# The causal mask of the diagonal score blocks, moved from TensorE to VectorE in a hybrid SSD and latent-attention kernel

## The chip, the cores and the metric

The kernel runs on one core of one Trainium2 chip. The metric is the device time of one execution in microseconds (us); the number of a kernel is the median of its runs. For the kernel before it is 1918.3 us, the median of three runs of 1915.88 to 1923.65.

## The reference, cut to what matters

The program is one inference step of a two-layer decoder trunk. The first layer is a Mamba-2 (SSD) mixer, the second a multi-head latent attention (MLA) with 16 heads. Both process a prompt of 1024 tokens and a sample group of 8 sequences with 8 new tokens each. The change touches the prompt's attention only, which in the reference is

```python
def latent_partial(q_lat, q_pe, ckv, kpe, mask):
    s = (jnp.einsum('bqhc,bkc->bhqk', q_lat, ckv.astype(F32))
         + jnp.einsum('bqhr,bkr->bhqk', q_pe.astype(F32), kpe.astype(F32))) * MLA_SCALE
    if mask is not None:
        s = jnp.where(mask, s, NEG_INF)
    m = jnp.max(s, axis=-1)
    p = jnp.exp(s - m[..., None])
    return m, jnp.sum(p, axis=-1), jnp.einsum('bhqk,bkc->bhqc', p, ckv.astype(F32))
```

called with the causal mask `q_pos >= k_pos`. A key later than its query must not count.

## The kernel before, in words

All matrix products run in fp32r, a rounded 32-bit type. To keep fp32 accuracy each operand is split into a rounded high part and a low remainder, and a product is made of three: high by high, high by low and low by high.

The program has these stages: the SSD layer, the projections of the MLA layer (`mla_in`, `mla_q`), the attention of the prompt head by head (`mla_heads`), and the sample group with the output projection (`mla_sample`). The change lies in the third.

`mla_heads` (L1492) loops over the 16 heads. A head has two query halves (`qc`, 512 queries each) and per half its key blocks of 128 (`jb`): 4 blocks for the first half, 8 for the second, 12 steps in all, `t` = 0 to 11. In each step it calls

- `qk` (L1424) for block `t`: three products into one of two PSUM buffers "st" (`HB[0]` is 2), scores with keys on the partitions and queries along the free axis. The query operand carries two more rows, minus the row maximum, so that the scores come out already shifted. Then two exponentials on ScalarE read that buffer: `th` (L1445), rounded to fp32r, and `P` (L1446), in fp32. Then `tl = P - th` (L1448) is the remainder of the probabilities. It is computed on GpSimd for odd `jb` and on VectorE for even `jb`.
- some units of other work: the row maxima of the next head (`maxpass`, L1390: one product "sc" and one masked maximum on VectorE, L1405 or L1407), and the preparation of the head after that (`prep`: transposes and splits of queries; for even heads keys too, and for every fourth head the values of four heads). These share four PSUM buffers "sc".
- `pv` (L1451) for the block two steps earlier (`LEAD` is 2): three products L1465, L1466, L1467 with the values, of which the third needs `tl`. After the last block of a half, ScalarE makes the reciprocal of the row sums as an exponential of a logarithm (`rl`, L1475 and L1477), VectorE multiplies by the gate (`og`, L1476), and GpSimd multiplies both (`og`, L1478). Because of the lead, the second half of a head ends in step `t` = 1 of the next head.

Where `jb >= 4 * qc` the key block meets the diagonal. Only the queries from its first key on are computed, so the four diagonal blocks of a half have 512, 384, 256 and 128 columns, and the first 128 columns need the causal mask. A head has 8 diagonal blocks. The mask, 0 or -1e30, is added by a fourth product (L1441), the identity times the mask, accumulated into the same buffer. Its two operands `mr` are rounded copies, made once in `Heads.start` (L1206, L1207).

The order of TensorE and GpSimd in this stage is that of the program text (`manual_schedule` in `layer_mla`). VectorE, ScalarE and the DMA queues get their order from the framework's scheduler when the program is built; each engine then runs its queue in that order.

Of the kernel before, what the change touches and what calls it, by code (L numbers as in the profile page):

```python
# [9 lines left out]
F32R = mybir.dt.float32r  # L10
AF = mybir.ActivationFunctionType
ALU = mybir.AluOpType
# [30 lines left out]
LEAD = 2  # L43
PF = 4
HB = (2, 4, 1, 2)
MDVE = False
SB = {"tr": 4, "sc4": 2, "on": 1, "pj": 1}
QG = 2
PRE = 4
# [66 lines left out]
def open_pool(tc, name, bufs=1, space=None, **kw):  # L116
    if space is None:
        return tc.tile_pool(name=name, bufs=bufs, reuse_waits="tile", **kw)
    if space == PS:
        return tc.tile_pool(name=name, bufs=bufs, space=space, reuse_waits="tile", **kw)  # L120
    return tc.tile_pool(name=name, bufs=bufs, space=space, **kw)
# [456 lines left out]
def bass_window(acc, start, stride, n):  # L578
    a = acc[:, :, start : start + (NB - 1) * stride + n]
    return bass.AP(a.tensor, a.offset, [list(a.ap[0]), list(a.ap[1]), [stride, NB], [1, n]])  # L580
# [572 lines left out]
def mla_q(k, st):  # L1153
    tc, nc, I = k.tc, k.nc, k.I
    wuq = I["mla_w_uq"][0].rearrange("q h e -> q (h e)")
    wp = st.enter_context(open_pool(tc, name="wpq", bufs=1, side="right"))
    sp = st.enter_context(open_pool(tc, name="spq", bufs=1, side="right"))
    ct, sn = k.rope
    for c in range(4):
        cs = slice(384 * c, 384 * c + 384)  # L1160
        wh, wl = load_w(k, wp if c % 2 else k.wu, wuq[:, cs], 4, 384, "wq", 1, k.wu, 1) if c else k.wu0
        for i, (t0, m) in enumerate(TILES):
            qt = sp.tile([128, 4, 96], F32, tag="qt", name=f"qt{c}{i}", bufs=2)
            qf = qt.rearrange("p h e -> p (h e)")
            p = k.psum.tile([128, 512], F32, tag="pj", name=f"pq{c}{i}", bufs=PB["pj"])
            drain(mm_tok(nc, p, m, 384, [(*both(k.cqh, k.cql, i, kk), wh[:, kk], wl[:, kk]) for kk in range(4)]))
            if m == 64:
                fold(nc, qf, p, 384)
            else:
                nc.scalar.copy(qf[:m], p[:m, :384])  # L1170
            u = sp.tile([128, 4, 2, 16], F32, tag="u3", name=f"u3{c}{i}", bufs=2)
            w = sp.tile([128, 4, 2, 16], F32, tag="w3", name=f"w3{c}{i}", bufs=2)
            cb = bass_bcast2(ct[:m, i], 4, 2)
            sb = bass_bcast2(sn[:m, i], 4, 2)
            pe = qt[:m, :, 64:96].rearrange("p h (a e) -> p h a e", a=2)
            nc.vector.tensor_tensor(u[:m], pe, cb, op=ALU.mult)
            nc.vector.tensor_tensor(w[:m], pe, sb, op=ALU.mult)
            nc.vector.tensor_tensor(pe[:, :, 0], u[:m, :, 0], w[:m, :, 1], op=ALU.subtract)
            nc.vector.tensor_tensor(pe[:, :, 1], u[:m, :, 1], w[:m, :, 0], op=ALU.add)
            nc.sync.dma_start(k.q_d[t0 : t0 + m, cs], qf[:m])  # L1180
            yield


class Heads:
# [16 lines left out]
        self.add_q(vp, 1)  # L1201

    def start(self, st):
        k, nc = self.k, self.k.nc
        self.sp = st.enter_context(open_pool(k.tc, name="q0", bufs=1))
        nc.vector.tensor_copy(k.mr[:, 0:128], k.ident)  # L1206
        nc.vector.tensor_copy(k.mr[:, 128:], self.maskt)  # L1207
        self.identr, self.masktr = k.mr[:, 0:128], k.mr[:, 128:]

    def load_mask(self):  # L1210
        nc = self.k.nc
# [212 lines left out]
    def qk(self, h, qc, jb):  # L1424
        k, nc, sp = self.k, self.k.nc, self.sp
        qh, ql = self.q_of(h)
        kh, kl = self.kT[h % NKT]
        o = max(0, jb - 4 * qc) * 128
        n = 512 - o
        ks = slice(128 * jb, 128 * jb + 128)  # L1430
        qs = slice(512 * qc + o, 512 * qc + 512)
        ps = self.psum.tile([128, 512], F32, tag="st", name=f"st{h}_{qc}_{jb}", bufs=HB[0])
        diag = jb >= 4 * qc
        nc.tensor.matmul(ps[:, :n], kh[:, ks], qh[:, qs], start=True, stop=False)  # L1434
        nc.tensor.matmul(ps[:, :n], kh[:, ks], ql[:, qs], start=False, stop=False)  # L1435
        nc.tensor.matmul(ps[:, :n], kl[:, ks], qh[:, qs], start=False, stop=MDVE or not diag)  # L1436
        if diag:
            if MDVE:
                nc.vector.tensor_tensor(ps[:, :128], ps[:, :128], self.maskt, op=ALU.add)
            else:  # L1440
                nc.tensor.matmul(ps[:, :128], self.identr, self.masktr, start=False, stop=True)  # L1441
        th = sp.tile([128, 512], F32R, tag="th", name="th", bufs=4)
        tl = sp.tile([128, 512], F32R, tag="tl", name="tl", bufs=3)
        P = sp.tile([128, 512], F32, tag="P", name="P", bufs=3)
        nc.scalar.activation(th[:, :n], ps[:, :n], AF.Exp, scale=SCALE)  # L1445
        nc.scalar.activation(P[:, :n], ps[:, :n], AF.Exp, scale=SCALE)  # L1446
        eng = nc.gpsimd if jb % 2 else nc.vector
        eng.tensor_tensor(tl[:, :n], P[:, :n], th[:, :n].bitcast(F32), op=ALU.subtract)  # L1448
        return th, tl

# [414 lines left out]
def mla_sample(k, sm, flow):  # L1865
    with ExitStack() as st:
        psum = st.enter_context(open_pool(k.tc, name="ps4", bufs=1, space=PS))
        out = MlaOut(k, st, psum, sm)
        sm.open(st, psum, out)
        sm.late_open(st)  # L1870
        k.sm = sm
        out.fill = fill = out.pieces(range(8))
        next(fill)
        drain(flow)
        last = None
        for x in TAIL:
            if x == "a":
                sm.turn_acc(NB - 1)
            elif x == "f":
                last = out.pieces((8,), sm.finish())  # L1880
            else:
                next(last if x == "s" else fill, None)
        drain(fill)
        drain(last)
# [138 lines left out]
def layer_mla(k):  # L2023
    tc, nc = k.tc, k.nc
    k.og_d = k.dram.tile([8, 128, SEQ], F32, name="og_d")
    k.npool = k.I["cache_ckv"].shape[1]
    with ExitStack() as st:
        k.q_d = k.dram.tile([T, MH * 96], F32, name="q_d")
        PB.update(PB2)
        k.cm = st.enter_context(open_pool(tc, name="cm", bufs=1))  # L2030
        right, mid, heads, k.mps = ExitStack(), ExitStack(), ExitStack(), ExitStack()
        p2 = ExitStack()
        k.psum = p2.enter_context(open_pool(tc, name="ps2", bufs=1, space=PS))
        k.psum.tile([128, 512], F32, tag="y", name="y2", bufs=PB["y"])
        mla_in(k, right, mid)
        k.qp = qp = st.enter_context(open_pool(tc, name="qp", bufs=1))
        k.qlh = qp.tile([128, 2, NB, 128], F32R, name="qlh")
        k.qll = qp.tile([128, 2, NB, 128], F32R, name="qll")
        k.qpr = qp.tile([96, NB, 128], F32R, name="qpr")
        k.mr = qp.tile([128, 256], F32R, name="mr")  # L2040
        early = ExitStack()
        hd = Heads(k, early)
        q0 = ExitStack()
        hd.start(q0)
        early_units = [hd.prep_kv(0)] * 13 + [hd.prep_q(0)] * 5 + [hd.maxpass(0, 0)] * 6
        early_units += [hd.prep_q(1)] * 5 + [hd.maxpass(0, 1)] * 10
        done = 0
        for n, _ in enumerate(mla_q(k, mid)):
            if n == 32:
                tc.keep_in_program_order(nc.scalar.preload_act_table_set("natural_log_exp_and_others"))  # L2050
            while done < min((n - Q0 + 1) * len(early_units) // (33 - Q0), len(early_units)):
                next(early_units[done], None)
                done += 1
        q0.close()
        mid.close()
        p2.close()
        psum = heads.enter_context(open_pool(tc, name="ps3", bufs=1, space=PS))
        hd.open(heads, psum)
        sm = Sample(k)
        with tc.manual_schedule(engines={nc.tensor.engine, nc.gpsimd.engine}):  # L2060
            flow = mla_heads(k, hd, sm, early, st)
        heads.close()
        right.close()
        with tc.manual_schedule(engines={nc.tensor.engine, nc.gpsimd.engine}):
            mla_sample(k, sm, flow)
        k.mps.close()
# [33 lines left out]
def hybrid_kernel(tc, ins, outs):  # L2100
    k = Ctx()
    k.tc, k.nc, k.I, k.O, k.ng = tc, tc.nc, ins, outs, G
    with ExitStack() as st:
        setup(k, st)
        layer_ssd(k)
        layer_mla(k)
# [19 lines left out]
```

## Time and profile before

| | |
|---|---|
| median of 3 runs | 1918.3 us |
| profiled execution, span | 1915.0 us |
| TensorE (PE) busy | 1887.4 us |
| VectorE (DVE) busy | 1208.5 us |
| ScalarE (ACT) busy | 1101.1 us |
| GpSimd (POOL) busy | 823.3 us |
| fourth product L1441 | 128 times, from 1309.6 to 1651.5 us |

The profile is of one execution. Its span runs from the first to the last instruction of the program; the time of a run also has what lies around it. A row of the lines view has the line, the engine, the operation, the tiles written and read, the shapes and the count, then the busy time, the mean of one in ns, and the idle time of the engine just before it with what ended that idle time. A row of the timeline has the start, the duration, the engine, the line and the tiles. PE is the matrix products and PEld the loads of their stationary operand. Products are pipelined, so that the duration of one is longer than the time until the next can start.

### The profile page before, as it was taken

To read this page: it belongs to the slowest core of one execution; us is meant where nothing else is said; L and a number is where in the kernel's file an instruction comes from. 1 tells how busy PE (TensorE), PEld (TensorE's weight loads), DVE (VectorE), ACT (ScalarE), POOL (GpSimd) and SP (SyncE) were. 2 spreads that over 40 slices of the span, in tenths; PEclk is the share of its full clock that TensorE was granted. 3 is DMA by queue.
4 is the path that set the end of the run, shared out by engine and by line. 5 is a ranking of instruction groups with operands and counts; after the bars stand their busy time and mean duration, and the time that the engine had idled before them with its cause. 6 is when DMAs were issued, how large, how long until landed. Compare 5 with 4: busy or idle time off the path is not lost.

```text
span 1915.0 us, 33672 instructions
## 1 busy us (share of the span) xinstructions
PE 1887.4 (99%) x12023; PEld 1728.1 (90%) x12023; DVE 1208.5 (63%) x2500; ACT 1101.1 (57%) x2528; POOL 823.3 (43%) x1116
## 2 busy tenths in 40 slices
PE   8999999999999999999999999999999999999998
PEld 7999999999999999888788998898888887888887
DVE  5557676757676767765534214566887878666665
ACT  6467666767666666732214323436777777755552
POOL 2447555555655555453004322103443434764551
PEclk9999999999999999999999999999999999999999
DMA  5223323332323232644424662233111112664451
GB/s 165 54 79 91 94 83 94 88 106 83 101 84 99 85 99 78 212 158 175 166 110 133 209 226 75 69 110 95 47 52 41 53 41 58 228 204 142 146 170 37
DMA packets 183967, 212.51 MB, mean 111 GB/s; under 512 B 19148, under 2 KB 147928, under 8 KB 182776
## 3 DMA queue, kind: packets, MB, share of 16 engines
q1 hardware_dynamic: 177304, 185.32, 31.1%
q0 software_dynamic: 6416, 24.91, 3.8%
q8 instruction: 95, 1.56, 0.3%
q14 instruction: 72, 0.59, 0.1%
q10 hardware_dynamic: 80, 0.13, 0.0%
HBM read 151.76 MB, written 58.52 MB: 110 GB/s over the span
## 4 chain that ended last, share of the span: by engine, by line
PE 90%; DMA 3%; DVE 3%; ACT 3%; issue 1%; POOL 0%; SPq 0%; POOLq 0%; DVEq 0%; ACTq 0%
PE pj L89 24%; PE pz L101 8%; PE pq L101 6%; PE pob L101 5%; PE p L101 5%; PE poa L101 4%; PE py L640 3%; PE sc L89 3%; PE o L89 2%; PE sc L1402 2%; PE o L1465 2%; PE o L1467 2%; PE st L1434 2%; PE st L1435 2%; PE st L1436 2%; PE o L1466 2%
## 5 line engine op out<-in xcount | busy, mean ns | idle before, releaser
L89 PE MATMUL pj<-xl,wih 128*128 128x384 f32 (+1 forms) x768 | 255.4, 333 | 0.0
L89 PE MATMUL pj<-xh,wih 128*128 128x384 f32 (+1 forms) x768 | 252.9, 333 | 1.2 <-ACT xh L276 0.8
L89 PE MATMUL pj<-xh,wil 128*128 128x384 f32 (+1 forms) x768 | 252.9, 329 | 0.0
L1448 POOL TENSOR_TENSOR tl<-P,th 128x384 fp32r<-128x384 f32 (+1 forms) x96 | 90.6, 944 | 232.3 <-ACT P L1446 186.6
L528 DVE SCALAR_TENSOR_TENSOR acc<-raw,vec,acc 128x1112 f32<-128x1112 f32 x96 | 141.6, 1476 | 15.3 <-ACT acc L524 14.4
L89 PEld LDWEIGHTS pj<-xh,wih 128*128 128x128 f32 x768 | 143.8, 188 | 2.6 <-ACT xh L276 1.4
L89 PEld LDWEIGHTS pj<-xl,wih 128*128 128x128 f32 x768 | 144.5, 188 | 1.0
L89 PEld LDWEIGHTS pj<-xh,wil 128*128 128x128 f32 x768 | 144.5, 188 | 0.5
L101 PE MATMUL pz<-wih,xh 128*128 128x256 f32 x504 | 143.3, 288 | 1.4 <-ACT z L569 1.4
L101 PE MATMUL pz<-wil,xh 128*128 128x256 f32 (+1 forms) x504 | 139.8, 283 | 0.0
L1445 ACT ACTIVATE th<-st 128x512 fp32r<-128x512 f32 x192 | 94.6, 493 | 66.6 <-PE st L1441 50.9
L101 PE MATMUL pz<-wih,xl 128*128 128x256 f32 x448 | 128.5, 287 | 0.0
L1733 POOL TENSOR_TENSOR kvl<-pgr,kvh 128x256 fp32r<-128x256 f32 x128 | 97.8, 791 | 70.6 <-ACT kvh L1731 70.3
L635 ACT ACTIVATE M<-M,tok 128x128 f32<-128x128 f32 (+1 forms) x288 | 90.4, 386 | 51.4 <-DVE M L631 51.2
L136 DVE TENSOR_TENSOR wil<-wraw,wih 128x512 fp32r<-128x512 f32 x88 | 74.4, 851 | 38.2 <-ACT wih L130 31.7
L101 PEld LDWEIGHTS pz<-wih,xh 128*128 128x128 f32 x504 | 95.9, 190 | 2.3 <-ACT z L569 1.8
L1446 ACT ACTIVATE P<-st 128x512 f32<-128x512 f32 x192 | 93.5, 487 | 0.0
L101 PEld LDWEIGHTS pz<-wil,xh 128*128 128x128 f32 (+1 forms) x504 | 92.8, 184 | 0.1
L101 PE MATMUL p<-w,oh 128*128 128x512 f32 (+3 forms) x304 | 88.8, 386 | 0.6 <-DVE h L1983 0.6
L616 POOL TENSOR_TENSOR xdd<-xsT,tok 128x256 f32<-128x256 f32 x64 | 50.0, 781 | 86.4 <-ACT xsT L602 83.3
L101 PEld LDWEIGHTS pz<-wih,xl 128*128 128x128 f32 x448 | 85.4, 191 | 0.7
L1448 DVE TENSOR_TENSOR tl<-P,th 128x512 fp32r<-128x512 f32 x96 | 72.1, 752 | 18.9 <-ACT P L1446 18.7
(830 smaller groups left out, 6212.5 us busy)
## 6 DMA issues: line engine op xcount, KB each, us to landing
wraw<-in_ssd_w_in SPq DMA_DIRECT2D x92, 256.0 KB
M<-acs_d SPq DMA_DIRECT2D x64, 256.0 KB
s<-in_state_ssm SPq DMA_DIRECT2D x32, 256.0 KB
y_d<-y SPq DMA_DIRECT2D x64, 128.0 KB
out_s_ssm<-s SPq DMA_DIRECT2D x32, 256.0 KB
q_d<-qt SPq DMA_DIRECT2D x32, 192.0 KB
qp<-q_d SPq DMA_DIRECT2D x8, 768.0 KB
wraw<-in_ssd_w_out SPq DMA_DIRECT2D x10, 512.0 KB
```

The source lines that it names most:

```text
L89: nc.tensor.matmul(out, a, b, start=(i == 0), stop=(i == n - 1))
L101: nc.tensor.matmul(o, a, b, start=(j == 0), stop=(j == len(ops) - 1))
L136: return (eng or nc.vector).tensor_tensor(lo, src, hi.bitcast(F32), op=ALU.subtract)
L528: last = nc.vector.scalar_tensor_tensor(acc, raw[:, j : j + n], k.convw[j][:, blk : blk + 1], acc, op0=ALU.mult, op1=ALU.add)
L616: nc.gpsimd.tensor_tensor(v3(xdd), v3(xsT), hb(2), op=ALU.mult)
L635: nc.scalar.activation(M[:m, h, :m], M[:m, h, :m], AF.Exp, bias=tk[:, 0, 4 * g + h : 4 * g + h + 1])
L640: nc.tensor.matmul(py[:m, h * 64 : h * 64 + 64], M[:m, h, :m], xsT[:m, h * 64 : h * 64 + 64], start=True, stop=True)
L1402: nc.tensor.matmul(ps[:, :n], qh[:96, 128 * i : 128 * i + 128], kh[:96, 512 * c : 512 * c + n], start=True, stop=True)
L1445: nc.scalar.activation(th[:, :n], ps[:, :n], AF.Exp, scale=SCALE)
L1446: nc.scalar.activation(P[:, :n], ps[:, :n], AF.Exp, scale=SCALE)
L1448: eng.tensor_tensor(tl[:, :n], P[:, :n], th[:, :n].bitcast(F32), op=ALU.subtract)
L1733: nc.gpsimd.tensor_tensor(rl[:, j], raw[:, j], rh[:, j].bitcast(F32), op=ALU.subtract)
```

## The change

The fourth product is gone. The third product ends the group, and VectorE then adds the fp32 mask `maskt`, which was in SBUF already, to the first 128 columns of the scores in PSUM, in place; the exponentials wait for that addition. The rounded copies of identity and mask are no longer made and their tile `mr` (1 KB per partition) is dropped, with the flag that chose between the two ways. The remainders `tl` of all diagonal blocks are computed on GpSimd, those with even `jb` too, which were on VectorE; the other blocks stay as they were.

```diff
@@ class Heads, start
-        k, nc = self.k, self.k.nc
+        k = self.k
         self.sp = st.enter_context(open_pool(k.tc, name="q0", bufs=1))
-        nc.vector.tensor_copy(k.mr[:, 0:128], k.ident)
-        nc.vector.tensor_copy(k.mr[:, 128:], self.maskt)
-        self.identr, self.masktr = k.mr[:, 0:128], k.mr[:, 128:]
@@ class Heads, qk
-        nc.tensor.matmul(ps[:, :n], kl[:, ks], qh[:, qs], start=False, stop=MDVE or not diag)
+        nc.tensor.matmul(ps[:, :n], kl[:, ks], qh[:, qs], start=False, stop=True)
         if diag:
-            if MDVE:
-                nc.vector.tensor_tensor(ps[:, :128], ps[:, :128], self.maskt, op=ALU.add)
-            else:
-                nc.tensor.matmul(ps[:, :128], self.identr, self.masktr, start=False, stop=True)
+            nc.vector.tensor_tensor(ps[:, :128], ps[:, :128], self.maskt, op=ALU.add)
...
-        eng = nc.gpsimd if jb % 2 else nc.vector
+        eng = nc.gpsimd if diag or jb % 2 else nc.vector
         eng.tensor_tensor(tl[:, :n], P[:, :n], th[:, :n].bitcast(F32), op=ALU.subtract)
@@ layer_mla
-        k.mr = qp.tile([128, 256], F32R, name="mr")
```

More of the change, by code (lines that the diff above doesn't have):

```diff
@@ L45 @@
 HB = (2, 4, 1, 2)
-MDVE = False
 SB = {"tr": 4, "sc4": 2, "on": 1, "pj": 1}
```

## The prediction

> **What bounds the kernel now.** I read the page first: the shares of the engines and the chain of work that ended last.
>
> ```profile
> span 1915.0 us, 33672 instructions
> PE 1887.4 (99%) x12023; PEld 1728.1 (90%) x12023; DVE 1208.5 (63%) x2500; ACT 1101.1 (57%) x2528; POOL 823.3 (43%) x1116
> ...
> PE 90%; DMA 3%; DVE 3%; ACT 3%; issue 1%; POOL 0%; SPq 0%; POOLq 0%; DVEq 0%; ACTq 0%
> ```
>
> TensorE is busy for 99% of the span and is 90% of the chain. The change lies in the stage of the attention heads, so I read that stage next: the windows view of the whole stage and of 50 us in its middle (columns: window, length, then busy time and instructions of PE, PEld, DVE, ACT, POOL, then clock and DMA), and the waits of PE in the stage.
>
> ```profile
> 1305.00:1655.00 350.00, 346.90 (x2023) 298.82 (x2023) 276.11 (x679) 264.65 (x599) 156.44 (x153) 1.00 0.22 64
> 1400.00:1450.00 50.00, 49.97 (x302) 43.65 (x301) 41.13 (x103) 39.14 (x89) 20.24 (x20) 1.00 0.18 50
> ```
>
> ```profile
> PE o L1467 <- POOL tl L1448: 1.3, 1, 1.3
> PE o L1467 <- DVE tl L1448: 0.9, 1, 0.9
> ```
>
> PE idles 0.03 us of 50 in mid-stage, at a granted clock of 1.00. Its few waits, 2.2 us in all, are for `tl`, the remainders that the change moves. VectorE is 82% busy (41.13 of 50), ScalarE 78%, GpSimd 40%. So each TensorE product removed shortens the time, and anything that makes `th`, `tl` or a score buffer late by more than its slack lengthens it.
>
> **What the change removes on TensorE.** The mask product runs 128 times (16 heads, 8 diagonal blocks each). What one costs can't be read from its busy time of 0.225 us, since products are pipelined; it is read from the starts. Its row in the tile view of the scores (least, median and largest ns), then the timeline of PE (start, duration): two 512-wide products, a block with the mask, a 128-wide block:
>
> ```profile
> L1441 PE MATMUL st<-mr x128: 221/225/278, 1309.6 to 1651.5; 128*128 128x128 f32 x128
> ```
>
> ```profile
> 1450.20 0.39 PE L1467 MATMUL o<-tl,Vh 128*128 128x512 f32 x1
> 1450.43 0.40 PE L1434 MATMUL st<-qTh,kTh 98*128 98x512 f32 x1
> ...
> 1453.10 0.39 PE L1436 MATMUL st<-qTh,kTl 98*128 98x512 f32 x1
> 1453.33 0.23 PE L1441 MATMUL st<-mr 128*128 128x128 f32 x1
> 1453.40 0.44 PE L89 MATMUL kp<-kvh,w 128*128 128x512 f32 x1
> 1453.68 0.40 PE L89 MATMUL kp<-kvl,w 128*128 128x512 f32 x1
> ...
> 1461.53 0.28 PE L1436 MATMUL st<-qTh,kTl 98*128 98x128 f32 x1
> 1461.64 0.28 PE L1441 MATMUL st<-mr 128*128 128x128 f32 x1
> ```
>
> A 512-wide product takes a slot of 0.23 us (1450.20 to 1450.43). With a mask product behind it, two 512-wide ones that should take 0.46 take 1453.10 to 1453.68, 0.58: the mask costs 0.12, of which 0.07 stands between its own start and the next, and 0.05 in the product after it, which starts late in effect. Among 128-wide products the slot is 0.11. I take 0.11: 128 x 0.11 = 14.1 us. Bounds: 0.07 gives 9.0, 0.12 gives 15.4. The lower one is what the chain counts, from start to start; I don't take it, because the 0.28 slot of the next product shows the rest.
>
> [...]
>
> The two casts that made the constant operands go as well:
>
> ```profile
> L1206 DVE CAST mr<-ident x1: 951/951/951, 1219.2 to 1219.2; 128x128 fp32r<-128x128 f32 x1
> L1207 DVE CAST mr<-mk x1: 1080/1080/1080, 1220.0 to 1220.0; 128x128 fp32r<-128x128 f32 x1
> ```
>
> They took 2.03 us of VectorE in the projections of the queries, and nothing waited for them (the views of these lines name no one). I cost them at nothing: PE was multiplying all through. If that cover were gone they would be worth 2 us, a gain.
>
> **What it adds and moves.** The remainders in the stage, shapes apart (busy time, mean ns), and the masked maxima by their line (least, median and largest ns):
>
> ```profile
> L1448 DVE TENSOR_TENSOR tl<-P,th 128x512 fp32r<-128x512 f32 x64 | 56.3, 880 | 18.8 <-ACT P L1446 18.7
> L1448 POOL TENSOR_TENSOR tl<-P,th 128x512 fp32r<-128x512 f32 x32 | 43.3, 1354 | 44.4 <-ACT P L1446 23.2 <-PE sc L1402 11.0 <-DVE nr L1419 4.5
> ...
> L1448 POOL TENSOR_TENSOR tl<-P,th 128x384 fp32r<-128x384 f32 x32 | 32.3, 1010 | 156.2 <-ACT P L1446 132.3 <-PE o L1467 23.7
> ...
> L1448 DVE TENSOR_TENSOR tl<-P,th 128x256 fp32r<-128x256 f32 x32 | 15.8, 494 | 0.1
> ...
> L1448 POOL TENSOR_TENSOR tl<-P,th 128x128 fp32r<-128x128 f32 x32 | 15.0, 468 | 31.7 <-ACT P L1446 31.1
> ```
>
> ```profile
> L1407 DVE CUSTOM_DVE_ANT_0 sc<-sc,mk x64: 276/490/733, 1259.2 to 1614.4; 128x128 f32<-128x128 f32 x16, 128x256 f32<-128x256 f32 x16, 128x384 f32<-128x384 f32 x16, 128x512 f32<-128x512 f32 x16
> ```
>
> The add of a 128x128 mask in PSUM has no row. The nearest is the narrowest form of L1407, 128x128: PSUM and the SBUF mask in, PSUM out, 0.276 us. I take 0.28. It can't be below nothing, as it is a new instruction; above, the subtraction of twice its width, 0.494. So 128 x 0.28 = 36 us (up to 63) are added to VectorE. Moved from it to GpSimd are the even diagonal blocks, 32 of 512 and 32 of 256: 32 x 0.88 + 32 x 0.494 = 44 us go from VectorE. On GpSimd they cost 32 x 1.354 + 32 x 0.74 = 67 us (0.74 is half way between its 468 at 128 and 1010 at 384). VectorE so loses 8 us (at worst gains 19), GpSimd goes from 156 to 223 of 350: no engine but PE becomes full on average. What counts is the delay in single chains.
>
> Such a chain was: last product, `th`, `P`, `tl`, then the third value product (L1467). Now the add stands before `th`, and `tl` of an even block takes longer. The add waits in VectorE's queue with the splits and maxima that free the four "sc" buffers behind it; `th` waits for it in ScalarE's queue, with the casts and the `rl` exponentials behind; PE waits for these in the end. In program order GpSimd does `tl` of blocks 0 and 1, `og` of the head before (L1478, 1.3 us), then blocks 2 and 3. Head 7, one of those with little preparation, in time order (start, duration):
>
> ```profile
> 1465.59 0.69 DVE L1448 TENSOR_TENSOR tl<-P,th 128x512 fp32r<-128x512 f32 x1 [0.47 <-ACT P L1446]
> ...
> 1466.42 0.34 PE L1434 MATMUL st<-qTh,kTh 98*128 98x256 f32 x1
> ...
> 1467.59 0.40 PE L1467 MATMUL o<-tl,Vh 128*128 128x512 f32 x1
> ...
> 1468.03 0.63 ACT L1477 ACTIVATE rl<-rl 64x512 f32<-64x512 f32 x1
> ...
> 1468.74 1.29 POOL L1478 TENSOR_TENSOR og<-og,rl 64x512 f32<-64x512 f32 x1 [1.14 <-PE sc L1402]
> ...
> 1470.20 0.28 PE L1467 MATMUL o<-tl,Vh 128*128 128x256 f32 x1
> ...
> 1475.28 1.28 POOL L1478 TENSOR_TENSOR og<-og,rl 64x512 f32<-64x512 f32 x1 [1.61 <-ACT rl L1477]
> ...
> 1475.36 1.75 DVE L1448 TENSOR_TENSOR tl<-P,th 128x512 fp32r<-128x512 f32 x1
> ```
>
> Block 0: `tl` ended at 1466.28 and was used at 1467.59, a slack of 1.31. The add (0.28) and GpSimd's 1.29 to 1.35 in place of 0.69 use 0.94; PE comes 0.22 earlier by two mask products gone. Slack left 0.15; I put 0.1 us of stall on each such head for a busy VectorE.
>
> Block 2: its `tl`, an even one, ran on VectorE, free of `og`. On GpSimd it follows `og`, which ends at 1470.03; 0.74 later is 1470.77, and PE wants it at 1470.20, 0.22 earlier by the products gone. That is a stall of 0.6 to 0.8; up to 1.1 if the add also pushes `P` and so the exponential behind it; only about 0.1 if ScalarE's planned order puts that exponential ahead of `th`, which would free `og` some 0.6 us sooner. I take 0.7. In an even head the same pair stands wide apart (head 6, columns as above):
>
> ```profile
> 1441.78 1.43 POOL L1478 TENSOR_TENSOR og<-og,rl 64x512 f32<-64x512 f32 x1 [1.41 <-PE o L1467]
> ...
> 1445.27 0.28 PE L1467 MATMUL o<-tl,Vh 128*128 128x256 f32 x1
> ```
>
> Here 1443.21 + 0.74 leaves over 1 us. So the stall falls on the seven odd heads 1 to 13, 7 x (0.7 + 0.1) = 5.6, and I put the same 0.7 on the two last, which have little to do between blocks: 1.4 (bounds 0, and twice 1.1 and some more for block 0, 3).
>
> The last two rows of head 7 show a VectorE subtraction held by GpSimd: `tl` took 1.75 instead of 0.69 while `og` ran. The add is not priced so: of the 64 masked maxima, with one operand in PSUM, the longest, at four times the width, took 0.733. [...] If the add were held as `tl` was, each would take 1.06 us more; the rows of the maxima speak against it.
>
> **The sum.** -14.1 + 5.6 + 1.4 = -7.1 us: the span goes from 1915.0 to 1907.9. The median of the runs is 1918.3, 3.3 above the profiled span, so 1911.2. A measurement of this kernel can tell about 0.5%, 9.6 us, from no change.
>
> **Rivals.** *The stalls don't come.* The exponential moves ahead, stalls sum to 2 us, and the gain is 12 to 13: 1906. For it: ScalarE has 22% free, and VectorE and ScalarE are planned anew; against: `og` alone takes 1.3 us of GpSimd just there.
>
> *The product was nearly free.* If it costs its 0.07 only, the gain is 9.0 less 7.0, 2 us: 1916. Against it is the 0.28 slot above. [...]
>
> *Slower: the add holds the score buffers.* There are two ("st"); `P` frees one. In head 7 `P` of block 0 ends as its `tl` starts, 1465.59, and block 2 takes the buffer at 1466.42, a slack of 0.83. An add that waits for one running VectorE instruction (0.69) and takes 0.28 is 0.97 late. If PE lost 0.2 us in each of the 128 blocks: 25.6 - 14.1 = +11.5, so 1930. It breaks even at 0.11 a block and is slower by 0.5% from 0.19. For it: VectorE at 82%. Against: in head 7 VectorE stood idle for 0.47 right there.
>
> **How the numbers follow.** Forecast 0.44 (own range 1908.7 to 1914); no stalls 0.35; nearly free 0.09; slower 0.12. So faster by over 0.5% 0.35; within 0.5% 0.53; slower 0.12. The lower end, 1902, is 1918.3 less 15.4 with no stall at all, rounded; the upper, 1925, reaches from the forecast over the nearly free product and half way into the slower rival.
>
> **What would show it.** No L1441 row; 128 VectorE adds of about 0.28 us; the slot after a block's third product 0.23 at once. Right: in odd heads PE waits at L1467 for a GpSimd `tl` behind `og`, 5 to 8 us in all, nearly none elsewhere. Wrong: PE waits at the first score product for `P` (buffers held), PE waits on "sc" buffers, or no waits at L1467.

## The result and the profile after

The changed kernel takes 1925.76 us (median of 5 runs, 1921.4 to 1927.35), the kernel before 1915.88 us in the same comparison (5 runs, 1914.28 to 1923.65). The ratio is 1.0041, with a 95% interval of 1.0025 to 1.0056: slower, though by less than the 0.5% that the prediction named as the limit of what can be told; a gain was forecast. Measured once more against 29 runs of the kernel before, the same program gave 1924.17 us, a ratio of 1.0036 (1.0023 to 1.0048). So about 7 us were lost where 7 were to be gained. One run of an experiment below, of the kernel before with a longer lead, took 3057.74 us at a granted clock of 0.56 and is left out of its median and ratio.

The page of the profile after: span, busy time, and the shares of the chain that ended last.

```profile
span 1925.6 us, 33687 instructions
PE 1884.9 (98%) x11895; PEld 1713.5 (89%) x11895; DVE 1204.7 (63%) x2562; ACT 1095.7 (57%) x2528; POOL 882.2 (46%) x1180
PE 84%; DMA 5%; DVE 4%; ACT 4%; POOL 2%; issue 1%; SPq 0%; POOLq 0%; DVEq 0%; ACTq 0%
```

TensorE is busy for 2.5 us less than before and the span is 10.6 us longer: TensorE waits. Its share of the chain fell from 90% to 84%, and GpSimd, at 0% before, has 2%.

The span needs care. Ahead of the heads both programs are the same but for two casts, yet the first score product of head 0 comes 6.0 us later than in the profile before. In the profiles of the twelve further runs it came 0.8 to 5.0 us later; four of those programs change nothing ahead of the heads, and they come 0.8 to 4.1 us later. So the profile before happens to be an execution that lost little up to there, and most of these 6 us are not the change's. From here on I match the products of both traces in order, from start to start, inside the heads only: by the first score product of the last head, the changed kernel has lost another 6.1 us, and by the last value product of the stage 7.4.

Windows over the stage of the heads and over 50 us of its middle (busy times of PE, PEld, DVE, ACT and POOL, then clock and DMA):

```profile
1315.00:1668.00 353.00, 338.53 (x1870) 280.16 (x1869) 276.27 (x736) 259.18 (x596) 217.52 (x217) 0.99 0.22 62
1412.00:1462.00 50.00, 49.16 (x286) 41.78 (x285) 41.82 (x115) 39.03 (x91) 29.30 (x30) 1.00 0.18 50
```

No engine but PE is full: VectorE 276 of 353 us, GpSimd 218. Yet PE, which idled 0.03 us of 50 in mid-stage before, now idles 0.84. The waits of PE in the stage, and then its products that waited longest, in order of time (in brackets the idle time before the product and who ended it):

```profile
PE o L1460 <- POOL tl L1441: 9.1, 10, 2.8
PE o L1460 <- DVE og L1469: 1.0, 1, 1.0
PE o L1460 <- DVE tl L1441: 1.0, 1, 1.0
PE nkp L1594 <- DVE nk L1591: 0.8, 1, 0.8
PE st L1430 <- ACT P L1439: 0.8, 2, 0.6
```

```profile
1346.56 0.39 PE L1460 MATMUL o<-tl,Vh 128*128 128x256 f32 x1 [2.77 <-POOL tl L1441]
1395.82 0.39 PE L1460 MATMUL o<-tl,Vh 128*128 128x256 f32 x1 [0.77 <-POOL tl L1441]
1436.04 0.39 PE L1460 MATMUL o<-tl,Vh 128*128 128x256 f32 x1 [0.71 <-POOL tl L1441]
...
1609.27 0.39 PE L1460 MATMUL o<-tl,Vh 128*128 128x256 f32 x1 [0.79 <-POOL tl L1441]
1630.03 0.39 PE L1460 MATMUL o<-tl,Vh 128*128 128x256 f32 x1 [1.19 <-POOL tl L1441]
```

These are the third value products of a block of 256 columns, block 2 of the first half: L1460 is the old L1467, `tl` is now L1441. One stands in each odd head, 0.68 to 0.79 us in heads 3 to 13, but 2.77 in head 1. The view of waits understates them. It counts idle time from the modelled end of the product before, 0.39 us after its start, while the next could have started after 0.23; and a wait below that difference of 0.16 isn't listed. From start to start over the whole stage, and without the half clock shown below, the third value products lose 11.8 us against before and the first score products 2.7.

Head 7, in time order, shows the ordinary case (the row ending in "x2" holds the `tl` of blocks 2 and 3):

```profile
1478.52 0.30 DVE L1434 TENSOR_TENSOR st<-st,mk 128x128 f32<-128x128 f32 x1 [0.53 <-PE st L1432]
...
1479.41 0.38 ACT L1439 ACTIVATE P<-st 128x256 f32<-128x256 f32 x1
1479.68 0.62 ACT L1470 ACTIVATE rl<-rl 64x512 f32<-64x512 f32 x1
...
1480.38 1.29 POOL L1471 TENSOR_TENSOR og<-og,rl 64x512 f32<-64x512 f32 x1 [0.60 <-ACT rl L1470]
1481.63 1.13 POOL L1441 TENSOR_TENSOR tl<-P,th 128x256 fp32r<-128x256 f32 x2
1482.40 0.38 PE L1460 MATMUL o<-tl,Vh 128*128 128x256 f32 x1 [0.78 <-POOL tl L1441]
```

`P` of block 2 is ready at 1479.79. GpSimd is idle then, but next in its queue stands `og`, which waits 0.60 us for the exponential `rl` that ScalarE does behind `P`. So `tl` of block 2 starts 1.84 us after its input was there. Head 1 has one thing more:

```profile
1342.01 1.03 POOL L1243 CAST kTh<-kTh 32x1024 fp32r<-32x1024 f32 x1
1342.99 1.03 POOL L1243 CAST kTl<-kTl 32x1024 fp32r<-32x1024 f32 x1
1344.11 1.27 POOL L1471 TENSOR_TENSOR og<-og,rl 64x512 f32<-64x512 f32 x1
1345.35 1.57 POOL L1441 TENSOR_TENSOR tl<-P,th 128x256 fp32r<-128x256 f32 x2
```

Two casts of rope keys (L1243, L1247 in the kernel before), 1.03 us each, stand ahead of `og`. Right behind that wait the granted clock is down, as the window of the next 10 us shows:

```profile
1350.00:1360.00 10.00, 10.00 (x41) 8.03 (x41) 6.07 (x14) 5.91 (x13) 7.06 (x8) 0.77 0.11 28
```

From 1347.8 on the clock is at half (0.50 in the window from 1350 to 1353) for 6.8 us, 4.6 of them in this window. That costs about half of its length, 3.4 us (an estimate). Not all of it is a loss against the kernel before, whose profile has 6.8 us of half clock as well, just behind the heads from 1673.2 on, where the profile after has none. The mean granted clock is 0.9974 over the 11 runs of the changed kernel and 0.9983 over 76 runs of the one before; on 1920 us the difference comes to 1.7 us, again an estimate.

### The profile page after: what moved, and what is told of

Its sections match the earlier page's. It is cut to its first block, busy times and chain, and to the rows that moved or that the text cites. A ratio compares the mean times of both kernels' runs of the same rounds, so it can differ in the third digit from the quotient of the medians.

```text
span 1925.6 us, 33687 instructions
## 1 busy us (share of the span) xinstructions
PE 1884.9 (98%) x11895; PEld 1713.5 (89%) x11895; DVE 1204.7 (63%) x2562; ACT 1095.7 (57%) x2528; POOL 882.2 (46%) x1180
## 4 chain that ended last, share of the span: by engine, by line
PE 84%; DMA 5%; DVE 4%; ACT 4%; POOL 2%; issue 1%; SPq 0%; POOLq 0%; DVEq 0%; ACTq 0%
PE pj L88 24%; PE pz L100 8%; PE pq L100 6%; PE pob L100 5%; PE p L100 5%; PE poa L100 3%; PE py L639 3%; PE sc L88 2%; PE o L88 2%; PE o L1460 2%; PE st L1430 1%; PE o L1458 1%; PE pk L100 1%; PE st L1432 1%; PE st L1431 1%
## 5 line engine op out<-in xcount | busy, mean ns | idle before, releaser
L1441 POOL TENSOR_TENSOR tl<-P,th 128x512 fp32r<-128x512 f32 (+3 forms) x160 | 154.1, 975 | 185.2 <-DVE mx L1403 84.9
L129 ACT CAST wih<-wraw 128x512 fp32r<-128x512 f32 x92 | 55.9, 616 | 45.2 <-PE pj L88 29.5
```

The source lines that it names most:

```text
L129: k.cast = nc.scalar.copy(hi, src)
```

## The experiments

Two theories. A: the loss is `tl` of the diagonal's even blocks, which in GpSimd's fixed order queues behind `og`, and in head 1 behind the key casts. B: the loss is the add. It stands between the scores and both exponentials and takes VectorE's room, so that `P` and VectorE's own results come late. A third question is what the product itself was worth. Ratios are against the kernel before on the same chip.

**The add alone, remainders where they were** (the changed kernel, with):

```diff
-        eng = nc.gpsimd if diag or jb % 2 else nc.vector
+        eng = nc.gpsimd if jb % 2 else nc.vector
```

> Mask added by VectorE, remainders divided as before (odd on GpSimd, even on VectorE). Theory A (the loss comes from even diagonal remainders queued on GpSimd behind og and, in head 1, behind the key casts): 10 to 14 us faster than before, near 1904; PE waits at the third value product fall from 11 us to 2 or 3. Theory B (the loss comes from the add standing before the exponentials): about as slow as the changed kernel, 5 to 10 us slower than before, and PE waits for P at the first score product.

1928.55 us, 1.0061 (1.0048 to 1.0074). A's forecast failed, and B's sign held: the add in place of the product loses without any move to GpSimd. The window of the stage, and the waits:

```profile
1312.00:1668.00 356.00, 338.98 (x1868) 277.39 (x1867) 305.20 (x800) 258.82 (x595) 155.36 (x152) 1.00 0.22 62
```

```profile
PE o L1467 <- DVE tl L1448: 5.6, 10, 0.8
PE nmp L1417 <- DVE nm L1414: 5.3, 13, 0.5
PE st L1434 <- ACT P L1446: 2.8, 7, 0.8
```

VectorE is at 305 of 356 us, 86%, and PE waits for what it makes: its `tl`, the maxima `nm`, and, through the exponentials, `P`.

But this run doesn't price the add, because more than the edit differs. VectorE's order is planned anew for each program. I compared the orders in the stage by the names of the instructions, adds and remainders left out: against the kernel before, 180 of 573 stand in another place here, most of them steps of the row maxima, and 28 in the changed kernel. The waits for `nm` may come from that plan.

**The remainders alone, product kept** (the kernel before, with the opposite edit):

```diff
-        eng = nc.gpsimd if jb % 2 else nc.vector
+        eng = nc.gpsimd if diag or jb % 2 else nc.vector
```

> The fourth product stays, only the even diagonal remainders go to GpSimd. Theory A: 8 to 14 us slower than before (0.6 us in each odd head, 2.5 us in head 1, a clock step of 3 us after it, 2 us in the last heads). Theory B: the same as before within 2 us.

1923.95 us, 1.0037 (1.0022 to 1.0051). PE's waits:

```profile
PE o L1467 <- POOL tl L1448: 5.9, 11, 1.7
```

So the move by itself costs some 7 us, too, and VectorE's order is nearly that of before (8 of 573 elsewhere). A is right about the move. What the add costs, the runs with zeros below tell. The two don't simply add up: the changed kernel has both and lost less than the run with the add alone.

**The mask product twice** (the kernel before; two equal products accumulated, so the mask is added twice):

```diff
-                nc.tensor.matmul(ps[:, :128], self.identr, self.masktr, start=False, stop=True)
+                for z in (False, True): nc.tensor.matmul(ps[:, :128], self.identr, self.masktr, start=False, stop=z)
```

> The mask product is issued twice, 128 products more, nothing else. If one costs 0.11 us of PE: 14 us slower, 12 to 16. If it costs only the 0.07 between the starts: 9 us or less. Either theory of the loss says the same.

1927.12 us, 1.0053 (1.0039 to 1.0067). The timeline of PE at a block with two 512-wide key products behind it:

```profile
1458.82 0.39 PE L1436 MATMUL st<-qTh,kTl 98*128 98x512 f32 x1
1459.06 0.34 PE L1441 MATMUL st<-mr 128*128 128x128 f32 x2
1459.23 0.45 PE L89 MATMUL kp<-kvh,w 128*128 128x512 f32 x1
1459.52 0.40 PE L89 MATMUL kp<-kvl,w 128*128 128x512 f32 x1
```

From 1458.82 to 1459.52 are 0.70 us; with one mask product the same stretch took 0.58, and in the changed kernel, with none, 0.46. So the slot is 0.12 here; in the median over the blocks it is 0.11, as was taken. In time, though, the second product costs 10.2 us (7.5 to 12.8), less than 128 x 0.11: a later PE finds fewer results late, and its third value products lose 3.2 us less by their starts.

**Block 2 back to VectorE** (the changed kernel):

```diff
-        eng = nc.gpsimd if diag or jb % 2 else nc.vector
+        eng = nc.gpsimd if (diag and jb % 4 == 0) or jb % 2 else nc.vector
```

> The changed kernel with the 256-wide diagonal remainders back on VectorE; the 512-wide diagonal ones stay on GpSimd. Theory A: the waits behind og go, 8 to 12 us faster than the changed kernel, 1906 to 1912 where before is 1916; head 1 shows no wait of 2.8 us and no half clock. Theory B: within 2 us of the changed kernel.

1925.41 us, 1.0038 (1.0025 to 1.0051): no better than the changed kernel, so A's forecast failed again. PE's waits:

```profile
PE o L1467 <- POOL tl L1448: 3.6, 4, 1.4
PE o L1467 <- DVE tl L1448: 3.3, 7, 1.0
PE nmp L1417 <- DVE nm L1414: 2.6, 7, 0.5
PE st L1434 <- ACT P L1446: 2.1, 3, 0.9
```

GpSimd's waits fell from 9.1 to 3.6, and VectorE's `tl` and `nm` came in their place. In head 1 A's forecast held: no third value product waits there, and no half clock follows. The queue behind `og` is real, but the work taken back by VectorE makes other results of that engine late.

**`og` later, remainders on GpSimd** (the changed kernel; GpSimd's product and its store are put off to steps 3 and 6):

```diff
-        nc.gpsimd.tensor_tensor(og[pj], og[pj], rl[pj], op=ALU.mult)
-        nc.sync.dma_start(k.og_d[pr, pj, cs], og[pj])
+
+        def late():
+            nc.gpsimd.tensor_tensor(og[pj], og[pj], rl[pj], op=ALU.mult)
+            nc.sync.dma_start(k.og_d[pr, pj, cs], og[pj])
+
+        self.late = late
...
+            if t in (3, 6) and getattr(hd, "late", None):
+                hd.late()
+                hd.late = None
...
+    hd.late()
```

> The changed kernel with og on GpSimd put behind the remainder of block 3 (or of block 6 of the second half) instead of before that of block 2; nothing added or removed. If block 2 was late because of og: the 0.85 us in each odd head go and the wait in head 1 shrinks, 6 to 9 us faster than the changed kernel, 1916 to 1920. If the add or VectorE makes it late: within 2 us of the changed kernel.

1916.3 us, 0.9986 (0.9977 to 0.9995). The same instructions in another order are 8 us quicker by the medians than the changed kernel, 10 by the ratios. Head 7, where the row with "x3" holds three `tl` back to back:

```profile
1467.20 3.09 POOL L1448 TENSOR_TENSOR tl<-P,th 128x512 fp32r<-128x512 f32 x3 [1.76 <-ACT P L1446]
...
1471.13 1.29 POOL L1480 TENSOR_TENSOR og<-og,rl 64x512 f32<-64x512 f32 x1
1471.15 0.28 PE L1467 MATMUL o<-tl,Vh 128*128 128x256 f32 x1
```

Block 2's `tl` is done before `og`, and its product has no wait. VectorE and ScalarE run in the changed kernel's order but for a handful of places, so the gain is that of GpSimd's queue. This shows A for the changed kernel.

**A zero add on top of the kernel before**, of 128 and of 8 columns (product and remainders as before; what is added are zeros):

```diff
                 nc.tensor.matmul(ps[:, :128], self.identr, self.masktr, start=False, stop=True)
+            nc.vector.tensor_tensor(ps[:, :128], ps[:, :128], self.maskr[:, 0:128], op=ALU.add)
```

The narrow one has, in place of the added line:

```diff
+            nc.vector.tensor_tensor(ps[:, :8], ps[:, :8], self.maskr[:, 0:8], op=ALU.add)
```

> The kernel before, fourth product and division of the remainders kept, and VectorE adds zeros to the same 128x128 scores in addition: the price of the add alone. By the prediction's sum it would cost 1 to 3 us (covered). By the run with the mask on VectorE alone, where 24 us were lost against 14 gained, it costs 10 to 18 us: 1927 to 1935.

> As the run that adds zeros to 128 columns, but to 8 columns: the same wait between score and exponential, a third or less of VectorE's time. If the wait in the chain costs: within 3 us of the 128-column run. If VectorE's room costs: at most a third of its loss, 1918 to 1923.

1924.07 us, 1.0028 (1.0019 to 1.0038) with 128 columns, and 1920.62 us, 1.0008 (0.9998 to 1.0018) with 8. The adds in the tile view (least, median, largest ns):

```profile
L1442 DVE TENSOR_TENSOR st<-st,mk x128: 277/299/331, 1313.0 to 1660.7; 128x128 f32<-128x128 f32 x128
```

```profile
L1442 DVE TENSOR_TENSOR st<-st,mk x128: 154/174/213, 1315.1 to 1660.5; 128x8 f32<-128x8 f32 x128
```

The wide add costs 5.4 us (3.6 to 7.3). The narrow one stands in the same place with the same waits, takes 58% of the time, and costs 1.5 (-0.4 to 3.5), which can't be told from nothing. So the price isn't only that of one more step and one more wait between scores and exponentials, which the narrow one has too. A price in proportion to the time of the adds would be 3.1 us for the narrow one, and these runs don't exclude it.

The traces tell more, with one profile of each. From start to start up to the last head, against the kernel before, the first score products, which wait for the exponentials, lose 2.0 us with the wide add and 2.2 with the narrow one. The products that wait for VectorE's maxima and keys ("nmp", "sc", "nkp") lose 3.2 and 0.5, the third value products lose 0.1 and gain 1.6. So what the wide add costs beyond the narrow one is VectorE's results coming late, in other words room on VectorE, of which the wide one takes 37 us and the narrow one 22.

**A longer lead, on the changed kernel and on the one before** (value products come three steps later instead of two; `qsn`, `wt` and `nr` give up their second buffer for the room; in the kernel before, the gate's tile `gt` does so too):

```diff
-LEAD = 2
+LEAD = 3
...
-        th = sp.tile([128, 512], F32R, tag="th", name="th", bufs=4)
-        tl = sp.tile([128, 512], F32R, tag="tl", name="tl", bufs=3)
+        th = sp.tile([128, 512], F32R, tag="th", name="th", bufs=5)
+        tl = sp.tile([128, 512], F32R, tag="tl", name="tl", bufs=4)
```

> The changed kernel with the value products three blocks behind the scores instead of two (one th and one tl buffer more, three small buffers single to make room). It gives tl a step of about 1.8 us more, but leaves the two score buffers as they are. If the loss is tl late at the third value product: those waits of PE (11 us) fall to 1 or 2 and it is 8 to 13 us faster than the changed kernel, 1912 to 1918 beside a before of 1917. If it is the score buffers or VectorE's room: within 3 us of the changed kernel.

> The kernel before with the longer lead alone (three blocks; the small buffers and the gate's single to make room). Its waits at the third value product were 2.2 us, so at most that is to be had: 0 to 3 us faster. If the lead were worth 4 us by itself, the gain of the changed kernel with the longer lead would not be the mask's.

The changed kernel with it: 1913.74 us, 0.9976 (0.9966 to 0.9985), 10 to 12 us below its runs without. The kernel before with it: 1914.88 us, 0.9984 (0.9975 to 0.9993). The waits of PE for GpSimd's `tl`, in the changed kernel and in the one before, both with the longer lead:

```profile
PE o L1467 <- POOL tl L1448: 1.4, 2, 0.8
```

```profile
PE o L1467 <- POOL tl L1448: 2.1, 2, 1.6
```

With one step more of slack these waits of the changed kernel fall from 9.1 us to 1.4, and its median is the lowest of all. But the lead helps the kernel before as well, and the two intervals overlap: that the mask on VectorE gains anything with the longer lead isn't shown.

**Both cures together** (the changed kernel with the longer lead and its buffers, and `og` put off as above, to later steps):

```diff
+            if t in (4, 7) and getattr(hd, "late", None):
+                hd.late()
+                hd.late = None
```

> The changed kernel with both the longer lead and og behind the remainders of the diagonal. With the lead alone 5.7 us were gained in the heads, with og late alone 3.6, of the 14 that the products cost; waits for P at the score buffers (2 to 3 us) stay. If the two cover the same waits: as the longer lead alone, 1913; if they add: 1908 to 1911.

1916.31 us, 0.9991 (0.998 to 1.0001). They don't add up. One wait in head 14 accounts for most of it in the profiled execution, with the half clock that comes with it:

```profile
PE o L1467 <- POOL tl L1448: 4.1, 2, 3.9
```

```profile
1622.16 1.25 POOL L1480 TENSOR_TENSOR og<-og,rl 64x512 f32<-64x512 f32 x1 [4.30 <-DMA pgr<-in_cache_ckv,ptidx]
1623.49 2.49 POOL L1448 TENSOR_TENSOR tl<-P,th 128x512 fp32r<-128x512 f32 x2
...
1624.81 0.79 PE L1467 MATMUL o<-tl,Vh 128*128 128x512 f32 x1 [3.85 <-POOL tl L1448]
```

Here GpSimd issues two gathers of cache pages for the sample group (`pgr`), and the `og` behind them then waits 4.30 us, by the profile until a gather has landed. The remainders stand behind that `og`: again a one-off in GpSimd's queue. The clock goes to half during the wait, at 1623.5, for 6.8 us.

**The changed kernel again, and with head 1's key casts on VectorE:**

```diff
-            (nc.vector if j == 1 else nc.gpsimd).tensor_copy(a[64:96], b[64:96].bitcast(F32))
+            (nc.vector if j in (1, 3) else nc.gpsimd).tensor_copy(a[64:96], b[64:96].bitcast(F32))
```

> The changed kernel once more (same program, lines kept in place). By its first runs 5 to 11 us slower than before; its own profile shows which part of the 6 us lost ahead of the heads, where both programs are the same, is chance.

> The changed kernel with the two casts of rope keys in head 1 (L1247, h = 3) on VectorE instead of GpSimd. If the 2.8 us wait of head 1 came from block 2's remainder queued behind these casts and og: the wait falls to about 0.8 and the half clock of 6.8 us after it goes, 3 to 6 us faster than the changed kernel. If not: within 1 us.

1924.17 us, 1.0036 (1.0023 to 1.0048), and 1921.09 us, 1.0012 (1.0003 to 1.0021). Two casts moved away are worth 3.1 us on the same chip: the wait in head 1 is 0.62 in place of 2.67, and the half clock behind it is gone. The orders of VectorE and ScalarE are otherwise the changed kernel's but for a handful of places. Head 1 with the casts on VectorE:

```profile
1339.79 1.29 POOL L1478 TENSOR_TENSOR og<-og,rl 64x512 f32<-64x512 f32 x1 [0.56 <-ACT rl L1477]
1341.04 1.13 POOL L1448 TENSOR_TENSOR tl<-P,th 128x256 fp32r<-128x256 f32 x2
1341.82 0.39 PE L1467 MATMUL o<-tl,Vh 128*128 128x256 f32 x1 [0.62 <-POOL tl L1448]
```

This is now the ordinary case of head 7.

One thing stays open. The add with the product (1.0028) lost less than the add without it (1.0061), though the second has 14 us less to do on PE by the 0.11 of a slot. PE's waits for VectorE account for it in kind. The second is also the run with the very different order of VectorE (180 of 573 places against 23 in the one with zeros in 128 columns), but whether the longer waits come from that plan or from PE's earlier demand wasn't tried.

## Why the prediction was wrong, point by point

*The product's slot, 0.11 us or 14.1 in all:* right for most blocks. The experiment with two products gives 0.12 between 512-wide ones. In the changed kernel's trace, though, the starts around the missing products come 12.2 us sooner in all: 0.11 each in most blocks, but 0.06 where a transpose of row maxima ("nmp") follows. And 0.11 is the gain on a PE that never waits. The second product cost 10.2 us, not 14.1, because slack came with it; the same slack goes when the product goes.

*The add, 0.28 us, and the engines' averages:* the durations were right, 0.298 each, 38.0 us in all, and GpSimd came to 218 us against 223. But VectorE was to lose 8 us and is where it was, 276.3 against 276.1. What moved away was cheaper than put:

```profile
L1441 DVE TENSOR_TENSOR tl<-P,th 128x512 fp32r<-128x512 f32 x32 | 33.9, 1059 | 6.2 <-ACT P L1439 6.1
```

The prediction took the mean of all 64 512-wide subtractions, 880 ns, for the 32 that moved. Matched block by block in the trace before, those took 704 and 724 ns, and with the 256-wide ones 38.6 us went and not 44. The two kinds that stayed took 713 and 1381, in the mean 1047, hardly less than the 1059 after: the slow one is block 2 of the second half, beside a busy GpSimd in both kernels. In head 7 after, it took 1.75 us, as in the prediction's row of before:

```profile
1482.70 0.68 DVE L1441 TENSOR_TENSOR tl<-P,th 128x512 fp32r<-128x512 f32 x1
...
1487.66 1.75 DVE L1441 TENSOR_TENSOR tl<-P,th 128x512 fp32r<-128x512 f32 x1
```

That such a subtraction is held while the add isn't, the prediction had from the rows of before, and the traces agree. In the one before, the 37 of the 512-wide subtractions that met no GpSimd instruction took 669 to 694 ns, and the 9 that ran beside one for over nine tenths of their time took 1463 in the mean. In the one after, the adds, 276 to 333 ns long, took 295 in the mean where GpSimd was busy throughout and 300 where it was idle. What it missed is that a mean over held and free ones prices neither.

*"No engine but PE becomes full":* true on average and of no help. With zeros added to 128 columns VectorE was at 86% and time was lost; what counts is the delay in single chains, as the next sentence of the prediction said.

*The stall, 7 x (0.7 + 0.1) + 1.4 = 7.0 us:* this is the step that failed, by size. Its mechanism was right to the place: block 2 of the odd heads, behind `og`, 0.68 to 0.79 us in heads 3 to 13 where 0.7 was put. Five things made it larger, all from start to start against before. First, head 1: two key casts stand ahead of `og` there, and 2.9 us are lost where 0.8 was put. The prediction read GpSimd's queue in head 7, named as one with little preparation, and carried it to head 1, whose queue holds a one-off. Second, the ordinary case by starts is 0.9 to 1.0 in each of heads 3 to 13, where 0.8 was put. Third, the last two heads lose 2.4 us in place of 1.4, and head 0, for which nothing was put, 0.7. Fourth, small losses that the forecast put at nothing: 2.7 us at the first score products and 1.6 at others. Fifth, the half clock, for which there was no term either: 3.4 us in this profile. So the third value products lose 11.8 us and the stage some 19.6 in all, where 7.0 was put. With the 12.2 gained at the missing products the sum is about +7.4, which is what the stage measured; forecast was -7.1.

*The rivals:* "slower" had the right sign and the wrong place. It was priced through the score buffers, which gave 2.7 us and not 25.6; what made the kernel slower was mainly the forecast's own stall, 4.8 us larger than put at the third value products, with the score products and the clock. With 0.12 it had too little weight: two parts of the change each cost time by themselves (7 us the move, 5.4 the add beside the product), which the forecast priced as one short stall and a covered add. That the exponential `rl` would move ahead of `th` didn't happen; in head 7 it is done behind `P`.

*The casts of the mask, at nothing:* nothing in the trace speaks against it.

*The offset of 3.3 us between span and median:* wrong as a rule. In every later profile the run's time is 1.7 to 2.1 us above its own span (1927.35 and 1925.6 after). The 3.3 held one execution's span against the median of three runs, and with two more that median is 1915.88.

## What to carry to other kernels

Before you move work to an engine with room, list what stands in that engine's queue between the input and the consumer, in each iteration, the first and the last and the ones with one-off work too: the share of busy time doesn't show it. An add on an engine that is 80% busy isn't free because one instance of it is covered (beside the product, 128 of them cost 5.4 us here); multiply it out and ask which of the engine's other results the bottleneck takes next. Price a piece that moves by its own rows and not by the mean of its group. If the slack is short, buy slack first, by a longer lead or a later place for work that nobody waits for, and then compare with the old kernel given the same slack.

## What the runs showed of the hardware

The three longest waits of PE for `tl` in these profiles are 2.67 us (the changed kernel again), 2.77 (the changed kernel) and 3.85 (both cures). With each the clock went to half, for 3.4, 6.8 and 6.8 us, in the third case during the wait and in the others 1.7 and 1.2 us behind it. Taking half of the half-clock time behind a wait as lost, which is an estimate, these waits cost 1.6 to 2.2 times their length.

For shorter waits it is a matter of the execution. Just behind the heads, all 14 profiles have one wait of 1.39 to 1.46 us for a remainder of the sample group; in the kernel before it is

```profile
1672.28 0.39 PE L89 MATMUL o<-kvh,pTl 128*128 128x256 f32 x1 [1.40 <-DVE pTl L136]
```

Within 0.9 us of it the clock goes to half for 6.8 us in three profiles, that of the kernel before among them, for 3.4 us in three, and not at all in eight, that of the changed kernel with its wait of 1.40 among them. So there is no clean limit in length: waits of 1.16 and 1.05 us had 3.4 us of half clock behind them, others of 1.57 and 1.68 none. All half clocks of the 14 profiles between 1300 and 1700 us began during a wait of PE of over 1 us or within 2.6 us of its end.

A VectorE addition in PSUM took 174 ns for 8 columns and 299 for 128 (medians of the two runs with zeros); a straight line through the two leaves 166 ns at no columns, an estimate, so by that line more than half of the wide one is a fixed cost.
